# A two-layer diffusion transformer with product-key experts: weight splits taken from GpSimd, a norm's scales moved into the choice of experts, gathered rows written over more chunks, and a modulation read from PSUM by two engines

## The chip, the cores and the metric

The kernel runs on one core of one Trainium2 chip. The metric is device time in microseconds (us), the median over runs of the whole program. The core has five engines with queues of their own: TensorE (PE in the profile, PEld for its weight loads), VectorE (DVE), ScalarE (ACT), GpSimd (POOL) and SyncE (SP). Transfers between HBM and SBUF are issued on the queues of SP, POOL and ACT; one engine waits for another by semaphores.

## The reference, cut to what matters

Two streams of 256 tokens (the latents `x` and a context `ctx`) with 1024 features go through two layers. Layer 0's mixer is latent attention beside bidirectional retention, layer 1's is a gated delta rule. Each is followed by a layer of experts with product keys (`peer`), and both have a modulation ahead and a post-norm behind. Only the latents of layer 1 are returned.

```python
for l in range(2):
    mod = silu(c) @ ada_w[l] + ada_b[l]            # six vectors: shift, scale, gate, twice
    h = x * (1 + sc1) + sh1                        # modulate; the context with its own vectors
    y = attn_retention(h) if l == 0 else deltanet(h)
    x = layer_norm(ALPHA * x + g1 * y) * ln1_g[l] + ln1_b[l]
    f = peer(x * (1 + sc2) + sh2)
    x = layer_norm(ALPHA * x + g2 * f) * ln2_g[l] + ln2_b[l]

def peer(h):                                       # per block of 128 tokens, 8 heads
    q = (h @ w_q).reshape(128, 8, 2, 128)
    v1, i1 = top_k(q[:, :, 0] . k1, 16); v2, i2 = top_k(q[:, :, 1] . k2, 16)
    sc, j = top_k(v1[..., :, None] + v2[..., None, :], 16)   # over 16 x 16 sums
    e = i1[j] * 128 + i2[j]                        # one of 16384 experts
    return sum(softmax(sc) * gelu(u_tab[e] . h) * v_tab[e])
```

## The kernel before, in words

**Precision.** All large products are made in 32 bits from two halves: `split` (L262) writes a rounded high half with ScalarE (L268) and the remainder `x - hi` as low half with VectorE or, where a caller says so, GpSimd (L271); `mm3` (L256) makes three matmuls of the four halves. So each weight costs a load, one ScalarE pass and one VectorE or GpSimd pass.

**Order.** The program is written as Python generators that `weave` and `pipe` interleave; this is the order of the text. The framework beneath then orders the instructions of each engine with a planner of its own, which uses modelled durations and takes the order of the text as priority, and sets the semaphores. Each engine works through its own list in order.

**First mixer** (`mixer0`, L468). Sixteen column blocks of the input weights (128x1024 each) are loaded and split by `weights` (L494), whose low halves (`arwl`) are made by GpSimd; 24 matmuls of 512 columns use each. The value projection of the retention (`ret_v`, L606) loads four more weights (`rvw`) through the same helper. Woven beside the sixteen projections are 24 `ada_unit`s (L333) with two instructions each: products of VectorE over a 128x1024 tile (`adaj`, L341), which make the modulation vectors of layer 0. `ret_v` follows alone (L630). Later the eight weights of the output projection (`wout`, L780) are split, every third low half by GpSimd.

**Norm and modulation.** `norm` writes the normalized x without its scale and shift; `modulate` (L430) folds both into the modulation's own scale and shift. For each of eight feature blocks TensorE transposes x into PSUM, VectorE scales it into the tile `hf` (L445), ScalarE copies that into the high half (L446), and VectorE and GpSimd by turns make the low half (L447). So x itself still lacks its scale and shift, which the residual needs: `affine` (L424) applies them, as two passes of GpSimd over each 128x1024 block, with rows that `norm_rows` (L388) loads over POOL's queue.

**Choice of experts** (`route`, L813). For each of 16 half heads: a projection (weights `wq` split with GpSimd making `usl`), a product with the keys, then VectorE's top 16 of each block's scores; after each second one, four sums of candidates (`cand`, L883) and a top 16 over them. `choose` (L889) pairs the projections with the top 16s and steps the dense layer's early chunks between. Then the choice is decoded and spread into a dense table of weights W in HBM (`spread`), while the remaining early chunks run. The early chunks (36 of 128 in layer 0, 24 in layer 1) are the products of expert rows `u` with the tokens, which don't need W.

**Dense layer** (`Dense.run`, L1148). All 128 chunks of 128 experts are gone through: the product with `u` and gelu where it wasn't made early, gelu times w (a slice of W, L1172), the split of both and of `v`, and the product with `v` (tile `f`) accumulated in PSUM. In layer 0 it does three blocks of tokens. The fourth block has its 128 chosen rows per token gathered (`Rows.steps`, L1057): per step one indirect load of a row of `u` and one of `v` on POOL's queue, one product of VectorE with `u` (`rowu`, L1072) and one accumulation with `v` (`rowy`, L1082), with `v` eight steps behind; 136 steps in all.

**What fills the dense loop** (`build`, L1711 on). A dictionary `fill` says what is written ahead of which chunk. `at(share)` finds the chunk at a share of the cost, which counts 18 for an early chunk and 36 for another, over 122 chunks. The 136 steps lie between 0.9 times the early share and 1, the 48 `ada_unit`s of layer 1 between the early share and 0.97, the affine of layer 0's four blocks (`affine`, L1731, called through `fill` at 0.4) in the middle, and the preparation of the gates ahead of chunk 124. Layer 1's dense loop has its own `affine` for two blocks, ahead of chunk 2.

Of the kernel before, what the change touches and what calls it, by code (L numbers as in the profile page):

```python
# [10 lines left out]
F32 = mybir.dt.float32  # L11
# [231 lines left out]
class Model:  # L243
# [186 lines left out]
    def modulate(self, pool, ps, l, m, x, s, hs, i0, ln):  # L430
        nc = self.nc
        sl = slice(i0 * P, (i0 + 2) * P)
        g, b = (self.c["ln_c"][:, ln[0], ln[1] - 1, z, :] for z in range(2))
        sc = pool.tile([P, KD], F32, tag="msc", name=f"msc{l}{m}{s}", bufs=2)
        sh = pool.tile([P, KD], F32, tag="msh", name=f"msh{l}{m}{s}", bufs=2)
        nc.vector.tensor_mul(sc, self.mod[l, m + 1][:, :, s], g)
        nc.vector.tensor_mul(sh, self.mod[l, m + 1][:, :, s], b)
        nc.vector.tensor_add(sh, sh, self.mod[l, m][:, :, s])
        for k in range(KD):
            self.n += 1  # L440
            o = ps.tile([P, 512], F32, tag="ps", name=f"xt{self.n}")
            for i in range(2):
                nc.tensor.transpose(o[:, i * P:(i + 1) * P], x[2 * s + i][:, k * P:(k + 1) * P], self.c["ident"])
            t = pool.tile([P, T], F32, tag="hf", name=f"hf{self.n}", bufs=3)
            nc.vector.tensor_scalar(t, o[:, :T], sc[:, k:k + 1], sh[:, k:k + 1], ALU.mult, ALU.add)  # L445
            nc.scalar.copy(hs[0][:, k, sl], t)  # L446
            (nc.gpsimd if k % 2 else nc.vector).tensor_sub(hs[1][:, k, sl], t, hs[0][:, k, sl].bitcast(F32))  # L447

# [19 lines left out]
    def mixer0(self, open_x, open_h):  # L468
# [25 lines left out]
        def weights(src, shape, nm):  # L494
            w = pw.tile(shape, F32, tag="w", name=nm, bufs=2)
            nc.sync.dma_start(w, src)
            return self.split(pw, w, shape, "arw", eng=nc.gpsimd)

# [120 lines left out]
        with ExitStack() as e2:  # L619
            pa = self.pool(e2, "m0ada2", 1, side="right")  # L620
            self.silu_rows(pa)

            def units():
                for m in (2, 3, 4):
                    for k in range(KD):
                        self.ada_unit(pa, 0, m, k, (0, 1))
                        yield

            weave(low(), pipe([key()] + [ret_proj(j) for j in range(4, 16)], 2), units())
            weave(ret_v())  # L630
        ep.close()
# [142 lines left out]
        with ExitStack() as e2:  # L774
            p = self.pool(e2, "m0o", 1, side="right")
            w = []
            for k in range(KD):
                r = p.tile([P, D], F32, tag="woutr", name=f"woutr{k}", bufs=3)
                nc.sync.dma_start(r, a["ar_out"][:, k, :])
                w.append(self.split(p, r, [P, D], f"wout{k}", eng=nc.gpsimd if k % 3 == 2 else nc.vector))  # L780
                next(rest, None)
# [30 lines left out]

    def route(self, l, hs, parts, ps, first, dense, e2, rows=None):  # L813
        nc, a, c = self.nc, self.a, self.c
# [15 lines left out]
        kT = p.tile([P, 16, P], F32, tag="A", name=f"kT{l}")  # L830
        nc.sync.dma_start(kT, a["p_k"][l])

        def top16(pool, vals, v, i, n, nm):
# [55 lines left out]
        def choose(part):  # L889
# [6 lines left out]
            while True:  # L896
                ends = [next(g, pr) is pr for g in (pr, tp)]
                if all(ends):
                    return
                if ends[0]:  # L900
                    n += 1
                    step(1 + n % 2)
                yield

# [109 lines left out]
        for part in range(len(parts)):  # L1014
            weave(choose(part))
        eq_.close()
        dense.by = None
# [646 lines left out]
def build(nc, tc, a, out, dbg=None, upto="all"):  # L1664
    es = ExitStack()
    with es:
# [38 lines left out]
        dense = m.Dense(m, 0, h, 3, *pools0, EARLY[0])  # L1705
        wd = m.route(0, h, ((0, 1, 2, 3),), ps, first, dense, e2, rows)
        ep.close()
# [8 lines left out]
        fill = {}  # L1716
        cost = np.cumsum([18 if c < EARLY[0] else 36 for c in range(NE - 6)])

# [6 lines left out]
        for i, u in enumerate(units):  # L1725
            n = 3 * KD
            share = ahead_share * (0.1 + 0.9 * i / n) if i < n else ahead_share + (0.97 - ahead_share) * (i - n) / (len(units) - n)
            fill.setdefault(at(share), []).append(lambda u=u: m.ada_unit(pa, *u))
        kept = {}

        def affine():  # L1731
            rows = m.norm_rows(pa, 0, 1, "adat")
            for t in x[:4]:
                m.affine(nc.gpsimd, t, rows)

# [3 lines left out]

        fill.setdefault(at(0.4), []).append(affine)  # L1740
        fill[0] = [lambda: m.silu_rows(pa)]
        fill[124] = [prepare]
        for i in range(P + LAG):
# [21 lines left out]
        with ed:  # L1765
            ep, ps = phase("r1ps")
            dense = m.Dense(m, 1, h, 2, *pools1, EARLY[1])
            wd = m.route(1, h, ((0, 1),), ps, first, dense, e2)
            ep.close()
# [6 lines left out]

            def affine():
                rows = m.norm_rows(pn, 1, 1)
                for t in x[2:4]:
                    m.affine(nc.gpsimd, t, rows)  # L1780

            last = dense.run(wd, *pools, {2: [affine]})
            for tb in range(2):
# [20 lines left out]
```

## Time and profile before

The median of three runs is 3058.61 us (3046.81, 3058.61, 3059.09). The profiled execution took 3056.68 us, of which its span, from the first to the last instruction, is 3054.9.

| | of the span |
|---|---|
| profiled execution, its span | 3056.68 us, 3054.9 us |
| TensorE busy | 2773.7 us, 91%, 16867 matmuls |
| VectorE busy | 2249.5 us, 74% |
| ScalarE busy | 1291.4 us, 42% |
| GpSimd busy | 643.4 us, 21% |
| granted clock of TensorE, mean | 0.955 |
| moved by DMA | 643.85 MB, 211 GB/s |

The stages follow one another: the first mixer's start and projections until 190 us, attention and retention until 300, its output projection until 371 with norm and modulation, layer 0's choice until 502, its decoding and the early chunks until 722, layer 0's dense loop until 1700, norm and modulation until 1736, the delta rule until 2157, layer 1's choice from 2170 to 2240, its table until 2360, its dense loop until 3035, and the last norm. A share of the whole span is an average over stages of different limits, so each is read by itself. In the view by stretches the busy times stand in the order TensorE, its weight loads, VectorE, ScalarE, GpSimd, each with its instructions in brackets; a clock of 1.00 is TensorE's full clock. A busy time counts an instruction from start to end, waiting for a shared resource included: the same instruction can show different durations in different stages.

### The profile page before, as it was taken

What the parts mean: (1) busy time and instruction counts of PE and PEld (TensorE: products, weight loads), DVE (VectorE), ACT (ScalarE), POOL (GpSimd) and SP (SyncE); (2) the same over time, 40 slices, a digit from 0 to 9 for tenths busy, and PEclk for the clock granted to TensorE, in tenths of its full rate; (3) what the DMA queues carried; (4) which work ended last, traced back from release to release, by engine and by line L of the source; (5) the groups of instructions that cost most, each with busy time, mean ns of one, the idle gap of its engine ahead of it and who ended that gap; (6) DMA issues with size and microseconds to landing.
All of it is one profiled execution on the core that took longest, in us unless ns stands there. A gap on an engine that the chain in (4) does not pass through costs nothing.

```text
span 3054.9 us, 44722 instructions
## 1 busy us (share of the span) xinstructions
PE 2773.7 (91%) x16867; PEld 2412.5 (79%) x16867; DVE 2249.5 (74%) x4414; ACT 1291.4 (42%) x2176; POOL 643.4 (21%) x413
## 2 busy tenths in 40 slices
PE   7988898987999789999999899678878899999997
PEld 4766788986788688888899677667877689999996
DVE  2976599796999898999744578876898655555555
ACT  3335333674333233333333356333457454444443
POOL 2410134001036765666100000122400100000000
PEclk9999899998999999999999899788999999999999
DMA  6531223668999799999744123313348866666763
GB/s 231 186 121 45 95 89 109 232 236 318 325 360 390 284 400 374 394 397 395 250 153 135 57 73 94 91 56 119 117 152 296 262 221 207 215 213 207 214 206 110
DMA packets 272168, 643.85 MB, mean 211 GB/s; under 512 B 36464, under 2 KB 138992, under 8 KB 267472
## 3 DMA queue, kind: packets, MB, share of 16 engines
q1 hardware_dynamic: 225120, 487.50, 47.7%
q0 software_dynamic: 38768, 142.49, 12.0%
q10 hardware_dynamic: 8064, 11.01, 1.0%
q8 instruction: 132, 2.16, 0.3%
q14 instruction: 84, 0.69, 0.1%
HBM read 583.77 MB, written 57.15 MB: 210 GB/s over the span
## 4 chain that ended last, share of the span: by engine, by line
PE 35%; DVE 13%; issue 9%; DMA 8%; POOL 5%; ACT 3%; POOLq 0%; DVEq 0%; ACTq 0%; SPq 0%
PE f L254 14%; PE act L254 13%; DMA rowv<-p_v,rowe 3%; PE dz L254 3%; DMA vr<-p_v 2%; POOL rowv L1065 2%; POOL rowu L1065 2%; DMA ur<-p_u 1%; DVE usl L271 1%; DVE vsl L271 1%; DVE cv L1332 1%; DVE rowu L1072 1%; PE qb L254 1%; DVE adaj L341 1%; DVE rowy L1082 1%
## 5 line engine op out<-in xcount | busy, mean ns | idle before, releaser
L254 PE MATMUL f<-vsl,gsh 128*128 128x512 f32 x1260 | 498.2, 397 | 29.2 <-DVE vsl L271 29.1
L254 PE MATMUL f<-vsh,gsh 128*128 128x512 f32 x1260 | 488.8, 397 | 23.7 <-ACT vsh L268 11.9
L254 PE MATMUL f<-vsh,gsl 128*128 128x512 f32 x1260 | 494.2, 394 | 7.0 <-DVE gsl L271 7.0
L271 DVE TENSOR_TENSOR vsl<-vr,vsh 128x1024 fp32r<-128x1024 f32 x252 | 304.2, 1239 | 193.9 <-ACT vsh L268 193.4
L271 DVE TENSOR_TENSOR usl<-ur,ush 128x1024 fp32r<-128x1024 f32 x240 | 293.8, 1225 | 182.4 <-ACT ush L268 180.8
L268 ACT ACTIVATE ush<-ur 128x1024 fp32r<-128x1024 f32 x256 | 270.3, 1056 | 268.5 <-PE act L254 165.9
L254 PE MATMUL act<-hp0h,usl 128*128 128x384 f32 x1024 | 348.1, 340 | 19.2 <-DVE usl L271 12.4
L254 PE MATMUL act<-hp0h,ush 128*128 128x384 f32 x1024 | 349.1, 341 | 3.6 <-ACT ush L268 3.3
L254 PE MATMUL act<-hp0l,ush 128*128 128x384 f32 x1024 | 346.7, 339 | 0.0
L268 ACT ACTIVATE vsh<-vr 128x1024 fp32r<-128x1024 f32 x252 | 257.6, 1053 | 207.9 <-PE f L254 141.1
L268 ACT ACTIVATE gsh<-gelu 128x384 fp32r<-128x384 f32 (+1 forms) x256 | 120.4, 471 | 490.7 <-DVE gelu L1172 380.7
L254 PEld LDWEIGHTS f<-vsl,gsh 128*128 128x128 f32 x1260 | 240.1, 191 | 85.9 <-DVE vsl L271 39.5
L254 PEld LDWEIGHTS f<-vsh,gsh 128*128 128x128 f32 x1260 | 238.6, 191 | 81.7 <-ACT vsh L268 22.8
L254 PE MATMUL act<-hp1h,usl 128*128 128x256 f32 x1024 | 292.6, 286 | 8.3 <-DVE usl L271 8.3
L254 PE MATMUL act<-hp1h,ush 128*128 128x256 f32 x1024 | 293.2, 286 | 1.3 <-ACT ush L268 1.2
L254 PE MATMUL act<-hp1l,ush 128*128 128x256 f32 x1024 | 292.3, 285 | 0.0
L254 PEld LDWEIGHTS f<-vsh,gsl 128*128 128x128 f32 x1260 | 240.0, 190 | 58.1 <-DVE gsl L271 8.4
L1065 POOL DMA_INDIRECT rowu<-p_ur,rowe x128 | 173.9, 1358 | 272.6 <-DVE rowa L1072 180.1
L254 PEld LDWEIGHTS act<-hp0h,usl 128*128 128x128 f32 x1024 | 195.0, 190 | 21.5 <-DVE usl L271 13.7
L1065 POOL DMA_INDIRECT rowv<-p_v,rowe x128 | 190.8, 1490 | 100.0 <-DVE rowy L1082 77.3
L254 PEld LDWEIGHTS act<-hp1h,usl 128*128 128x128 f32 x1024 | 198.4, 194 | 9.4 <-DVE usl L271 9.2
L254 PEld LDWEIGHTS act<-hp1h,ush 128*128 128x128 f32 x1024 | 198.7, 194 | 3.8 <-ACT ush L268 1.7
(777 smaller groups left out, 5810.8 us busy)
## 6 DMA issues: line engine op xcount, KB each, us to landing
ur<-p_u SPq DMA_DIRECT2D x256, 512.0 KB
vr<-p_v SPq DMA_DIRECT2D x256, 512.0 KB
adat<-ada_t SPq DMA_DIRECT2D x80, 512.0 KB
W<-wst SPq DMA_DIRECT2D x20, 2048.0 KB
w<-W SPq DMA_DIRECT2D x32, 768.0 KB
wq<-p_wq SPq DMA_DIRECT2D x32, 512.0 KB
dw<-dn_in SPq DMA_DIRECT2D x32, 512.0 KB
w<-W SPq DMA_DIRECT2D x32, 512.0 KB
```

What stands on the lines that cost most here:

```text
L254: self.nc.tensor.matmul(out, l, r, start=start, stop=stop)
L268: nc.scalar.activation(hi, x, AF.Copy)
L271: (eng or nc.vector).tensor_sub(lo, x, hi.bitcast(F32))
L341: nc.vector.tensor_tensor_reduce(j, w, self.crow[:, s, :], op0=ALU.mult, op1=ALU.add, scale=1.0, scalar=self.c["ada_c"][:, l, m, k:k + 1], ...
L1065: nc.gpsimd.indirect_dma_start(t, None, tabs[z], bass.IndirectOffsetOnAxis(ap=self.e[:, s:s + 1], axis=0))
L1072: nc.vector.tensor_tensor_reduce(u, u, self.h, op0=ALU.mult, op1=ALU.add, scale=1.0, scalar=0.0, accum_out=self.act[:, s:s + 1])
L1082: nc.vector.scalar_tensor_tensor(self.y, rows.pop((1, v)), self.g[:, v:v + 1], self.y, ALU.mult, ALU.add)
L1332: (nc.gpsimd if CONV[j] == "p" else nc.vector).scalar_tensor_tensor(co, xp[:, :ns, q:q + T], cw[:, j, q:q + 1], co, ALU.mult, ALU.add)
```

## The change

In seven places:

1. `modulate`: ScalarE makes the high half from the transposed block in PSUM with scale and bias, instead of copying VectorE's result; VectorE makes all low halves.
2. `weights` in the first mixer: the low halves are made by VectorE (the default of `split`).
3. The `ada_unit`s of the first mixer: 16 of 24 are woven beside the projections, the rest three at a time beside `ret_v`.
4. The output weights: all low halves by VectorE.
5. `route` gets `x` and a generator `scaled`, which loads the scale and shift on POOL's queue and applies them to each block with GpSimd; `choose` takes one of its passes every fourth turn, and what is left is taken at the end. It runs in both layers.
6. The two `affine`s in `build` are gone.
7. The cost of `at` runs over 126 chunks instead of 122, the `ada_unit`s of layer 1 end at 0.87 instead of 0.97, and the entry at chunk 124 is added to what stands there.

```diff
@@ modulate
-            nc.scalar.copy(hs[0][:, k, sl], t)
-            (nc.gpsimd if k % 2 else nc.vector).tensor_sub(hs[1][:, k, sl], t, hs[0][:, k, sl].bitcast(F32))
+            nc.scalar.activation(hs[0][:, k, sl], o[:, :T], AF.Identity, bias=sh[:, k:k + 1], scale=sc[:, k:k + 1])
+            nc.vector.tensor_sub(hs[1][:, k, sl], t, hs[0][:, k, sl].bitcast(F32))
@@ mixer0
-            return self.split(pw, w, shape, "arw", eng=nc.gpsimd)
+            return self.split(pw, w, shape, "arw")
...
-            weave(low(), pipe([key()] + [ret_proj(j) for j in range(4, 16)], 2), units())
-            weave(ret_v())
+            sums = units()
+            weave(low(), pipe([key()] + [ret_proj(j) for j in range(4, 16)], 2), islice(sums, 2 * KD))
+            weave(ret_v(), until=sums, steps=3)
...
-                w.append(self.split(p, r, [P, D], f"wout{k}", eng=nc.gpsimd if k % 3 == 2 else nc.vector))
+                w.append(self.split(p, r, [P, D], f"wout{k}"))
@@ route
-    def route(self, l, hs, parts, ps, first, dense, e2, rows=None):
+    def route(self, l, hs, parts, ps, first, dense, e2, x, rows=None):
...
+        def scaled():
+            gb = p.tile([P, 2, D], F32, tag="A", name=f"lgb{l}")
+            for i, z in enumerate("gb"):
+                nc.gpsimd.dma_start(gb[:, i, :], a[f"ln1_{z}"][l])
+            for t in x:
+                nc.gpsimd.tensor_mul(t, t, gb[:, 0, :])
+                yield
+                nc.gpsimd.tensor_add(t, t, gb[:, 1, :])
+                yield
+
+        scale = scaled()
@@ choose
+                n += 1
                 if ends[0]:
-                    n += 1
                     step(1 + n % 2)
+                if n % 4 == 0:
+                    next(scale, None)
                 yield
...
             weave(choose(part))
+        weave(scale)
@@ build
-        wd = m.route(0, h, ((0, 1, 2, 3),), ps, first, dense, e2, rows)
+        wd = m.route(0, h, ((0, 1, 2, 3),), ps, first, dense, e2, x[:4], rows)
...
-        cost = np.cumsum([18 if c < EARLY[0] else 36 for c in range(NE - 6)])
+        cost = np.cumsum([18 if c < EARLY[0] else 36 for c in range(NE - 2)])
...
-            share = ahead_share * (0.1 + 0.9 * i / n) if i < n else ahead_share + (0.97 - ahead_share) * (i - n) / (len(units) - n)
+            share = ahead_share * (0.1 + 0.9 * i / n) if i < n else ahead_share + (0.87 - ahead_share) * (i - n) / (len(units) - n)
...
-        def affine():
-            rows = m.norm_rows(pa, 0, 1, "adat")
-            for t in x[:4]:
-                m.affine(nc.gpsimd, t, rows)
...
-        fill.setdefault(at(0.4), []).append(affine)
-        fill[124] = [prepare]
+        fill.setdefault(124, []).append(prepare)
...
-            wd = m.route(1, h, ((0, 1),), ps, first, dense, e2)
+            wd = m.route(1, h, ((0, 1),), ps, first, dense, e2, x[2:4])
...
-            def affine():
-                rows = m.norm_rows(pn, 1, 1)
-                for t in x[2:4]:
-                    m.affine(nc.gpsimd, t, rows)
-
-            last = dense.run(wd, *pools, {2: [affine]})
+            last = dense.run(wd, *pools, {})
```

## Rows read from the trace of the kernel before

**Rows 1.** Busy time by stretches: us, busy per engine (count), clock, DMA share, GB/s
```profile
70.00:180.00 110.00, 98.78 (x433) 80.37 (x432) 107.15 (x153) 32.14 (x44) 44.60 (x16) 0.95 0.53 179
384.00:502.00 118.00, 112.37 (x573) 97.91 (x571) 115.66 (x807) 37.62 (x55) 42.29 (x18) 0.99 0.26 86
1000.00:1070.00 70.00, 52.80 (x252) 46.75 (x250) 54.57 (x59) 15.94 (x23) 50.13 (x31) 0.91 0.75 272
1070.00:1480.00 410.00, 387.63 (x1906) 347.58 (x1907) 382.53 (x522) 138.01 (x207) 244.71 (x171) 0.97 1.02 387
1500.00:1690.00 190.00, 190.00 (x983) 173.83 (x982) 75.98 (x90) 70.44 (x97) 0.00 (x0) 1.00 0.46 143
```

**Rows 2.** Timeline of GpSimd, 1010 to 1070: start, us, line, instruction, [idle before, releaser]
```profile
1017.34 2.49 POOL L425 TENSOR_TENSOR x<-x,lg 128x1024 f32<-128x1024 f32 x1 [8.43 <-DMA lg<-ln_g]
...
1049.86 13.13 POOL L426 TENSOR_TENSOR x<-x,lb 128x1024 f32<-128x1024 f32 x4 [5.12 <-DMA lb<-ln_b]
```

**Rows 3.** Timeline of VectorE, 1046 to 1066
```profile
1050.69 6.74 DVE L271 TENSOR_TENSOR vsl<-vr,vsh 128x1024 fp32r<-128x1024 f32 x2
```

**Rows 4.** Groups by line of VectorE, 1070 to 1480: busy us, mean ns, idle before
```profile
L1082 DVE SCALAR_TENSOR_TENSOR rowy<-rowv,rowg,rowy 128x1024 f32<-128x1024 f32 x90 | 115.7, 1285 | 22.4 <-DMA rowv<-p_v,rowe 21.9 <-DVE rowg L1079 0.5
L1072 DVE CUSTOM_DVE_ANT_0 rowu<-rowu,rowh 128x1024 f32<-128x1024 f32 x85 | 103.8, 1221 | 0.0
...
L271 DVE TENSOR_TENSOR vsl<-vr,vsh 128x1024 fp32r<-128x1024 f32 x46 | 54.2, 1221 | 0.0
L341 DVE CUSTOM_DVE_ANT_0 adaj<-adat,c_row,small 128x1024 f16<-128x1024 f32 x21 | 26.9, 1279 | 0.0
L1172 DVE TENSOR_TENSOR gelu<-gelu,w 128x384 f32<-128x384 f32 x46 | 25.5, 554 | 7.0 <-ACT gelu L1137 7.0
```

**Rows 5.** Chain of waits, 2340 to 2400: start, us, what
```profile
2360.06 13.68 DMA w<-W
2373.76 5.41 DVE gelu L1172 x3
2379.17 2.49 DVE gsl L271
```

**Rows 6.** Timeline of GpSimd, 2350 to 2390
```profile
2371.55 4.85 POOL L425 TENSOR_TENSOR xl<-xl,lg 128x1024 f32<-128x1024 f32 x2 [8.81 <-DMA lg<-ln_g]
2376.36 5.01 POOL L426 TENSOR_TENSOR xl<-xl,lb 128x1024 f32<-128x1024 f32 x2
```

**Rows 7.** Timeline of VectorE, 2370 to 2390
```profile
2382.24 1.08 DVE L1172 TENSOR_TENSOR gelu<-gelu,w 128x256 f32<-128x256 f32 x3
```

**Rows 8.** Groups by line of GpSimd, 20 to 210
```profile
L271 POOL TENSOR_TENSOR arwl<-arw,arwh 128x1024 fp32r<-128x1024 f32 x16 | 43.2, 2699 | 92.9 <-ACT arwh L268 85.6 <-PE z L254 7.3
```

**Rows 9.** Groups by line of VectorE, 60 to 210
```profile
L341 DVE CUSTOM_DVE_ANT_0 adaj<-adat,c_row,small 128x1024 f16<-128x1024 f32 x48 | 79.1, 1648 | 13.5 <-ACT c_row L330 12.3 <-DMA adat<-ada_t 0.6
```

**Rows 10.** Instructions of L603: durations min/median/max in ns
```profile
L603 DVE TENSOR_TENSOR rq<-rq,rcos x4: 409/1340/2303, 105.1 to 128.7; 128x256 f32<-128x256 f32 x4
```

**Rows 11.** Who waited for tile arwl: us, times
```profile
  PE rvp L254: 3.2, 2
  PE z L254: 1.6, 1
```

**Rows 12.** Instructions of L883: durations min/median/max in ns
```profile
L883 DVE TENSOR_TENSOR cand<-V x64: 164/200/2419, 394.7 to 2234.3; 128x32 f32<-128x32 f32 x24, 128x64 f32<-128x64 f32 x16, 128x96 f32<-128x96 f32 x8, 128x48 f32<-128x48 f32 x8
```

**Rows 13.** Timeline of GpSimd, 2170 to 2185
```profile
2176.92 2.40 POOL L271 TENSOR_TENSOR usl<-wq,ush 128x1024 fp32r<-128x1024 f32 x1 [0.91 <-ACT ush L268]
```

**Rows 14.** Instructions of L447: durations min/median/max in ns
```profile
L447 DVE TENSOR_TENSOR hp0l<-hf,hp0h x16: 415/426/427, 349.7 to 1734.8; 128x256 fp32r<-128x256 f32 x16
L447 POOL TENSOR_TENSOR hp0l<-hf,hp0h x16: 715/732/1182, 350.2 to 1735.4; 128x256 fp32r<-128x256 f32 x16
```

**Rows 15.** Instructions of L513: durations min/median/max in ns
```profile
L513 ACT ACTIVATE h0h<-xT,mod,mod x16: 589/592/602, 45.9 to 53.3; 128x256 fp32r<-128x256 f32 x16
```

**Rows 16.** Busy time of tile rowy by stretch: DVE, POOL, clock, DMA share, GB/s
```profile
1500.00:1690.00 190.00, 0.00 (x0) 0.00 (x0) 1.00 0.46 143
```

## The prediction, made before the changed kernel was run

> **What bounds the kernel now.** I read the busy time by stretches first, then the groups by line inside each stretch, then the waits of one tile and the timeline where a group's mean hid a few long instructions. The profiled execution took 3056.68 us (its span is 3054.9), 1.9 us below the median of the runs, 3058.61; the sum is made against 3056.68.
>
> The stretches have different bounds [rows 1]. From 1500 to 1690, layer 0's dense loop without anything woven in, TensorE is busy 190.0 of 190 us at full clock: 983 matmuls, 5.17 per us. From 1070 to 1480, the same loop with the gathered rows, VectorE is busy 382.5 of 410 and TensorE makes 1906 matmuls, 4.65 per us: VectorE leads there. From 1000 to 1070 both fall: 252 matmuls, 3.60 per us, with the clock at 0.91. In layer 0's choice of experts (384 to 502) VectorE is busy 115.7 of 118. In the first mixer's projections (70 to 180) it is busy 107.2 of 110, TensorE 98.8.
>
> **Layer 0's scales leave the dense loop.** Eight GpSimd passes over a 128x1024 tile stand at 1017 to 1063: one alone 2.49 us (three more like it), the last four together 13.13 [rows 2], so 23 us. VectorE's instructions that run beside them are held: two vsl splits took 6.74 us [rows 3], where one takes 1.22 [rows 4]. From 1000 to 1070 TensorE made 73 matmuls fewer than at the rate of 1070 to 1480 (4.65 x 70 = 325 against 252), worth 73 / 4.65 = 15.8 us. So the gain lies between 15.8 (what TensorE shows inside the window) and 23 (all of GpSimd's passes, with the gathers queued behind them on POOL's queue). I take 20, past the middle, because the gathers delayed at 1063 cost a little behind the window too. The cover of this work is gone with it: what is late next is VectorE's own load, as in 1070 to 1480. **-20.**
>
> **Layer 1's scales leave its dense loop.** Here the passes sit on the chain of waits: w (the table of weights) lands at 2373.74 after 13.68 us, three gelu products take 5.41 us, one gsl 2.49, and GpSimd's four passes run from 2371.55 to 2381.4 [rows 5, 6]. Three such products without a neighbour take 1.08 us [rows 7], 0.36 each. So 5.41 - 1.08 = 4.3 and 2.49 - 0.36 = 2.1 go: 6.4. Two of the four 0.5 MB loads of scales issued beside w go as well, an estimate of 1.05 MB / 387 GB/s [rows 1] = 2.7 us. Between 6.4 and 9.1; below that if the next vr loads are late anyway. I take 8. **-8.**
>
> **The first mixer's splits.** Twenty weight splits of 128x1024 leave GpSimd (16 at a mean of 2.70 us [rows 8], and four more of the same shape) for VectorE, at 1.22 each as vsl [rows 4]: +24.4 us there. What VectorE gets back is its waiting beside GpSimd. Its 48 ada products have a mean of 1.648 us [rows 9] against 1.279 in the dense loop [rows 4]: 17.7 us; rotary products of 0.41 go up to 2.30 [rows 10]. So VectorE's sum changes by +6.7 or, with the rotary ones, by about nothing. TensorE's own waits for arwl are 3.2 and 1.6 us [rows 11] and go in part. Ends: +6.7 (VectorE's added time at the stage's end) and -11.2 (all of TensorE's idle time from 70 to 180 [rows 1]). I take the 4.8 less a little. Eight of the 24 ada units are written beside the v projection now; they are the filler of VectorE in either place. **-4.**
>
> **The choices get twelve passes.** Eight (layer 0) and four (layer 1), each some 2.4 us, and two 0.5 MB loads each on POOL's queue ahead of them. The first pass of x waited 8.43 us for its load [rows 2], and whatever stands behind it on POOL, the splits of wq that TensorE needs, waits too. VectorE's top-16 instructions read one tensor; those that read two can be held: a cand sum has a median of 0.20 us and a maximum of 2.42, a whole GpSimd pass [rows 12]. In layer 0 POOL is busy 42.3 of 118 us [rows 1] and 8 x 2.4 + 8.4 = 28 fit into the rest, with at most two cand sums held: 0 to +5. In layer 1 POOL has 0.91 us between splits [rows 13]: each pass pushes the next split by 2.4 - 0.9 = 1.5, four by 6, and the load's wait beyond one period of 3.3 adds 5: 0 to +11. VectorE sees it only when the scores come late, so I take a third of 16. **+5.**
>
> **Modulation.** Per stream of eight blocks, VectorE takes four more differences of 0.43 us, 1.7; GpSimd's, 0.73 each, leave [rows 14] the chain. ScalarE's instruction grows to that of 0.59 us with scale and bias [rows 15], and ScalarE has room (37.6 busy of 118 even beside it [rows 1]). Five streams: between +8.5 (all of VectorE's) and -6.0 (4 x 0.30 x 5). TensorE's k-by-k start hides most of either. **0.** The Trainium skill speaks against a gain here: "PSUM — Partial Sum Buffer", section "PSUM bank collisions raise a hardware error", says that two engines may not use one bank and quadrant at once, two reads included. By it ScalarE's read has to stand behind VectorE's of the same transposed block and the chain stays as long as it is; without it each stream would begin up to one scaling on VectorE earlier. No row shows two engines on one PSUM tile at a time.
>
> **Output weights.** Two of eight splits move (GpSimd to VectorE); that stretch waits for the loads. Between -1 and +2.4, taken as **0**.
>
> **Pacing.** The steps of the gathered rows were written at 136 over chunks 32 to 121, 1.5 per chunk. The trace has 90 rowy and 46 vsl in 410 us [rows 4]: 1.96 per chunk, and none after 1500 [rows 16], 19 chunks before the text's end. So the order on VectorE isn't that of the text: the framework's planner puts ready work that is written later into time that it counts as free. Four more chunks of text change nothing in that, nor does an ada share of 0.87 (21 units per 46 chunks in the trace, 18 as written). I take **0**; the other end is priced as the first rival, -41. A loss is bounded by the steps left over at the end, 2.6 us each.
>
> **Sum.** -20 - 8 - 4 + 5 + 0 + 0 + 0 = -27: 3056.7 - 27 = 3029.7, **3030 us**. With each term at its nearer end, 3015 to 3043.
>
> **Rivals.**
> *The pacing holds.* If the steps stay where they are written, two chunks of VectorE cost 2 x (1.22 + 1.22 + 0.55 + 0.55) = 7.1, 2.9 steps x (1.285 + 1.221 + 0.08) = 7.5, 0.84 ada x 1.36 = 1.1 [rows 4]: 15.7 us, under TensorE's 2 x 42 matmuls / 5.17 = 16.2. Then 1070 to 1480 runs at TensorE's rate: 410 - 1906 / 5.17 = 41.3 go [rows 1]. Time: 2988. Against it: the rate of 1.96, the same before and after the pause at 1000. 12%.
> *The choices eat it.* The twelve passes land on VectorE's chain at their full 16 us, and layer 1's gain shrinks to 4 because its loop is then fed late: 3030 + 11 + 4 = 3045. For: POOL's 0.91 us in layer 1, and the wait of 8.43 for a load that the planner had not foreseen. Against: in layer 0 VectorE consumes slower (118 / 16 = 7.4 us per head half) than POOL's queue supplies (42.3 / 16 = 2.6 now, 4.4 with the passes and the load's wait). 22%.
> *VectorE becomes the bound of the first mixer.* It is busy 107.2 of 110 us already. If each projection's low half is ready only after one ada product and its own split, 1.28 + 1.22 = 2.5 us past TensorE's need, 20 x 2.5 = 50 us are lost instead of 4 gained: 3030 + 54 = 3084, slower than before. It decides as soon as the split starts later than the third matmul of its projection; today's two splits of lead (24 matmuls each, 24 x 98.78 / 433 = 5.5 us [rows 1]) speak against it, VectorE's in-order queue for it. 9%.
> The forecast itself has 57%.
>
> **How the numbers follow.** About 0.5%, 15 us, is what can be told from no change here: faster is below 3043, slower above 3074. The forecast's 57% and the paced rival's 12% lie below, less some 3% of the forecast's upper tail, plus 2% of the second rival: 68% faster. The second rival's rest and that tail: 22% the same (1% to the rival's other side). The third rival and mishaps: 10% slower. The range takes in the paced rival and the second one, 2986 to 3054, and leaves out the third and the tails; the forecast's own range is 3015 to 3043.
>
> **What would show it.** Right: no POOL pass inside the two dense loops; 1000 to 1070 at 4.6 matmuls per us; gelu products of 0.36 us at the start of layer 1's loop; ada products at 1.28 in the first mixer; some 4 rowy per two chunks still, ending about 19 chunks before the loop does. Wrong: rowy present up to the last chunks (first rival); idle VectorE in the choices ended by ScalarE's S (second); TensorE's idle time in 70 to 180 ended by VectorE's arwl (third). The prediction as a whole is wrong if the loop of 1070 to 1480 changes its rate, since every other term is small beside that.

## The result

The changed kernel takes 3023.64 us (median of 4 runs, 3018.56 to 3027.8) against 3058.85 before: a ratio of 0.9891 with a 95% interval of 0.9866 to 0.9915. Predicted were 3030, in a range of 2986 to 3054, and faster with 68%. The profiled execution took 3025.72 us with a span of 3024.0, 30.9 below the span of before.

To see where they went, the traces are cut at the same instructions of TensorE. The table is worked out from the start times of its first or last matmul into the tile named in brackets (`rvp` belongs to the value projection, `q` to the attention, `xt` to the transposes of the modulation, `pq` to the choice of experts, `f` to the dense layer, `dz` and `yo` to the delta rule). The column of before has the length of each stage in us; every other entry is the length of that stage less its length before, so that a row with the same number in several kernels is one effect. The kernels E1 to E12 are the experiments below.

| stage, from its first to the next one's first matmul | before | after | E1 | E2 | E3 | E4 | E5 | E6 | E7 | E12 |
|---|---|---|---|---|---|---|---|---|---|---|
| start and 16 projections (to `rvp`) | 157.9 | -4.7 | +0.5 | -4.4 | -0.8 | +1.5 | -3.8 | -5.4 | -5.3 | -4.0 |
| value projection (to `q`) | 30.4 | -7.3 | +0.4 | -7.3 | 0 | -0.1 | -7.3 | -7.3 | -7.3 | -7.3 |
| attention, output projection (to `xt`) | 159.7 | +2.0 | -0.3 | +1.3 | 0 | +2.7 | +3.2 | +3.1 | +0.9 | +1.4 |
| norm, modulation of layer 0 (to `pq`) | 20.4 | +6.7 | 0 | 0 | +1.4 | 0 | 0 | 0 | +1.5 | +6.4 |
| choice, table (to `f`) | 359.0 | -1.3 | +3.9 | -4.9 | -3.8 | -5.3 | -5.5 | +5.4 | -0.2 | -4.3 |
| dense loop of layer 0 (to `dz`) | 1009.0 | -18.8 | -18.3 | +5.1 | +4.0 | +2.2 | +5.1 | -20.4 | -10.6 | -60.4 |
| delta rule (to the last `yo`) | 412.7 | +2.4 | +1.4 | +1.8 | +3.8 | +0.6 | +2.5 | +1.9 | -0.5 | +0.9 |
| norm, choice, table of layer 1 (to `f`) | 225.7 | -1.7 | +0.3 | -1.0 | -2.1 | +0.3 | +5.5 | +1.2 | -6.8 | -2.1 |
| dense loop of layer 1 (last `f`) | 662.4 | -7.8 | -4.0 | -1.7 | -1.3 | +0.7 | -0.9 | -7.1 | -6.5 | -7.3 |
| rest | 17.9 | -0.4 | -0.4 | -0.2 | -0.2 | -0.2 | -0.2 | -0.4 | -0.2 | -0.4 |

E8, E9, E10 and E11, which the table leaves out, have +76.1, +54.9, +55.5 and +73.6 in the dense loop of layer 0.

How far one execution can be trusted is read from the columns whose edit lies elsewhere. E2 to E5 all have 4 to 6 us less between `pq` and `f` and 2 to 5 more in the loop behind: the border between these two stages lay late in the one execution of before, and their sum, 1368.0, moves by no more than 3.1 in them. The rows of layer 1 vary by up to 5.5, and the attention by 2.7 in E4, whose edit lies behind it.

Now the views of the kernel after. The busy time by stretches, where the fourth to last column is GpSimd (with instructions), then clock, DMA share and GB/s, answers to [rows 1]:

```profile
996.00:1066.00 70.00, 67.02 (x336) 59.81 (x335) 66.67 (x90) 25.04 (x38) 41.24 (x31) 1.00 1.04 398
1066.00:1476.00 410.00, 388.02 (x1918) 346.48 (x1918) 375.99 (x509) 138.04 (x206) 226.10 (x164) 0.99 1.00 376
1476.00:1666.00 190.00, 190.00 (x984) 173.81 (x983) 75.85 (x90) 70.40 (x97) 0.00 (x0) 1.00 0.45 143
```

In the 70 us that answer to 1000 to 1070 TensorE makes 336 matmuls, 4.80 per us instead of 3.60, at a clock of 1.00 instead of 0.91: GpSimd's passes are gone from there. The next 410 us are as they were, 1918 matmuls against 1906. The tile `rowy` is as empty at the loop's end as in [rows 16]:

```profile
1476.00:1666.00 190.00, 0.00 (x0) 0.00 (x0) 1.00 0.45 143
```

In layer 1 the first gelu products take 0.36 us each, where three took 5.41 [rows 5]; VectorE's timeline:

```profile
2351.02 1.09 DVE L1189 TENSOR_TENSOR gelu<-gelu,w 128x256 f32<-128x256 f32 x3
```

The passes went further forward than the text has them. The timelines of GpSimd and of VectorE at layer 0's second modulation, in columns as in [rows 2]:

```profile
356.29 4.83 POOL L840 TENSOR_TENSOR x<-x,lgb 128x1024 f32<-128x1024 f32 x2 [3.26 <-ACT x L421]
361.08 5.02 POOL L842 TENSOR_TENSOR x<-x,lgb 128x1024 f32<-128x1024 f32 x2
366.06 5.08 POOL L840 TENSOR_TENSOR x<-x,lgb 128x1024 f32<-128x1024 f32 x2
375.36 2.40 POOL L271 TENSOR_TENSOR usl<-wq,ush 128x1024 fp32r<-128x1024 f32 x1 [4.22 <-ACT ush L268]
```

```profile
356.07 1.45 DVE L445 TENSOR_SCALAR hf<-xt,msc,msh 128x256 f32<-128x256 f32 x3 [1.84 <-PE xt L443]
357.43 6.45 DVE L447 TENSOR_TENSOR hp0l<-hf,hp0h 128x256 fp32r<-128x256 f32 x3
363.80 1.44 DVE L445 TENSOR_SCALAR hf<-xt,msc,msh 128x256 f32<-128x256 f32 x3
365.16 6.26 DVE L447 TENSOR_TENSOR hp0l<-hf,hp0h 128x256 fp32r<-128x256 f32 x3
```

The text puts the first pass into the choice, which starts at 365.0; GpSimd made it at 356.3, as soon as x was normalized. Three differences of VectorE take 6.45 us beside them, 2.15 each, against 0.43 [rows 14], and TensorE's first projection waits 7.5 us. The Trainium skill ("SBUF — State Buffer", section "Summary: rules for kernel authors") says that of a VectorE instruction with two inputs in SBUF and a GpSimd one that reads SBUF the later waits until the other is done; these durations agree, each about one GpSimd pass of 2.4 us.

### The profile page after: what moved, and what is told of

Read it like the earlier page. It is cut to its first block, busy times and chain, and to the rows that moved or that the text cites. A ratio compares the mean times of both kernels' runs of the same rounds, so it can differ in the third digit from the quotient of the medians.

```text
span 3024.0 us, 44724 instructions
## 1 busy us (share of the span) xinstructions
PE 2772.1 (92%) x16867; PEld 2411.1 (80%) x16867; DVE 2242.3 (74%) x4456; ACT 1293.5 (43%) x2176; POOL 552.2 (18%) x371
## 4 chain that ended last, share of the span: by engine, by line
PE 38%; DVE 13%; DMA 11%; issue 8%; ACT 4%; POOL 3%; POOLq 0%; SPq 0%; ACTq 0%; DVEq 0%
PE f L254 15%; PE act L254 14%; DMA rowv<-p_v,rowe 3%; DMA ur<-p_u 3%; PE dz L254 3%; DMA vr<-p_v 3%; POOL rowv L1082 1%; POOL rowu L1082 1%; DVE vsl L271 1%; DVE usl L271 1%; DVE rowu L1089 1%; DVE rowy L1099 1%; DMA w<-W 1%; DVE cv L1349 1%; PE wp L254 1%
## 5 line engine op out<-in xcount | busy, mean ns | idle before, releaser
L254 PEld LDWEIGHTS act<-hp1l,ush 128*128 128x128 f32 x1024 | 199.1, 194 | 2.8 <-issue 0.6
```

What stands on the lines that cost most here:

```text
L254: self.nc.tensor.matmul(out, l, r, start=start, stop=stop)
```

## The experiments

All times are medians, and the ratios are to the kernel before on the same chip. They are named E1 to E12 in the order of their labels.

**E1, the scales alone.**

```diff
-        fill.setdefault(at(0.4), []).append(affine)
...
-            last = dense.run(wd, *pools, {2: [affine]})
+            last = dense.run(wd, *pools, {})
...
+                if n % 4 == 0:
+                    next(scale, None)
```

> Of the change only the move of the scales from the two dense loops into the two choices, everything else as before. Theory (read from the two traces): the passes run earlier than the text has them, beside the second modulation of layer 0, and hold VectorE's low halves there: the time from the first transposed block to the first projection of the choice grows by 7 us (it grew from 20.4 to 27.2 with the whole change), layer 0's dense loop loses 19 to 20, layer 1's choice grows by 2 to 5, layer 1's dense loop loses 11; in all -20 from 3058 = 3038. Rival: those 7 us come from the modulation's own edit; then that stretch stays at 20.4 here and the whole is -27 = 3031.

3038.05 us, ratio 0.9924 (0.9902 to 0.9946). The total is what the theory said, 3038, but its terms are not. The stretch to `pq` stays at 20.4, which was the rival's sign, so the 7 us there need a second edit; and layer 1 has -4.0 in its loop and +0.3 in its choice, where -11 and +2 to +5 were expected. Here the passes run at 378.9 and later, in the choice, and TensorE pays there. The timeline of GpSimd, then TensorE's waits (us, times, longest):

```profile
378.90 4.75 POOL L839 TENSOR_TENSOR x<-x,lgb 128x1024 f32<-128x1024 f32 x2 [5.16 <-DMA lgb<-ln_g]
383.61 4.66 POOL L841 TENSOR_TENSOR x<-x,lgb 128x1024 f32<-128x1024 f32 x2
388.22 2.34 POOL L839 TENSOR_TENSOR x<-x,lgb 128x1024 f32<-128x1024 f32 x1
390.51 2.34 POOL L271 TENSOR_TENSOR usl<-wq,ush 128x1024 fp32r<-128x1024 f32 x1
```

```profile
PE pq L254 <- POOL usl L271: 9.0, 2, 8.8
```

The split `usl` at 390.51 stands behind five passes on GpSimd's queue, and the projection that needs it waits 8.8 us. The eight passes cost about as much as in the changed kernel (+3.9 in the choice, against +6.7 - 1.3 = 5.4 for both stages there); only the victim is another.

**E2, the first mixer alone** (its splits and the order of the units).

```diff
-            return self.split(pw, w, shape, "arw", eng=nc.gpsimd)
+            return self.split(pw, w, shape, "arw")
...
-            weave(low(), pipe([key()] + [ret_proj(j) for j in range(4, 16)], 2), units())
-            weave(ret_v())
+            sums = units()
+            weave(low(), pipe([key()] + [ret_proj(j) for j in range(4, 16)], 2), islice(sums, 2 * KD))
+            weave(ret_v(), until=sums, steps=3)
```

> Of the change only the first mixer: its twenty weight splits by VectorE and the order of the 24 units. Theory: the gain of 12 us up to the last matmul of the value projection (10 up to the output projection) belongs to this part alone, 4.7 of it ahead of the value projection; the rest of the program keeps its length: 3058 - 10 = 3048. Rival from the prediction (VectorE becomes the bound): the projections end later, above 3060.

3046.28 us, ratio 0.9956 (0.9942 to 0.9969). The theory holds: 11.7 us less up to `q`, and the rival that VectorE becomes the bound is out.

**E5, the splits without the order of the units.**

```diff
-            return self.split(pw, w, shape, "arw", eng=nc.gpsimd)
+            return self.split(pw, w, shape, "arw")
```

> Of the change only the twenty splits of the first mixer by VectorE; the 24 units all stay beside the projections. With splits and units together the last matmul of the value projection came 11.8 us earlier, 4.4 of it ahead of that projection and 7.4 in it. Theory: the 7.4 come from the splits (TensorE waited there for GpSimd's arwl), so here too the value projection takes 21.5 instead of 28.9 us, and the whole is 3061 - 10 = 3051. Rival: the order of the units makes them; then the projections end later here with 24 units in them, and at least 5 of the 11.8 us are gone: 3056 or more.

3051.73 us, ratio 0.9962 (0.9938 to 0.9986). Its first two stages, -3.8 and -7.3, are within 0.6 of those of E2 (-4.4 and -7.3): the splits make the gain. The 0.6 is less than what the first row moves by in E3 and E4, whose edits lie elsewhere (-0.8 and +1.5), so a gain by the order of the units isn't shown.

**E3, the modulation alone.**

```diff
-            nc.scalar.copy(hs[0][:, k, sl], t)
-            (nc.gpsimd if k % 2 else nc.vector).tensor_sub(hs[1][:, k, sl], t, hs[0][:, k, sl].bitcast(F32))
+            nc.scalar.activation(hs[0][:, k, sl], o[:, :T], AF.Identity, bias=sh[:, k:k + 1], scale=sc[:, k:k + 1])
+            nc.vector.tensor_sub(hs[1][:, k, sl], t, hs[0][:, k, sl].bitcast(F32))
```

> Of the change only the modulation: ScalarE makes the high half from PSUM, VectorE all low halves. Theory: 0 within 1 us in each of the three places (first transposed block to first projection stays 20.4 +- 1 in layer 0), the whole 3058 +- 5; ScalarE's instruction on a block begins only when VectorE's on the same block has ended. Rival: this edit is what took 7 us ahead of layer 0's choice: that stretch is 27 here and the whole 3065.

3063.49 us, ratio 1.0011 (0.9993 to 1.0029): no difference. The stretch is 1.4 longer, not 7 (and 1.5 longer in E7, which has this edit and no passes there). ScalarE's group in it (mean ns, idle time, releaser):

```profile
L446 ACT ACTIVATE hp0h<-xt,msh,msc 128x256 fp32r<-128x256 f32 x16 | 7.9, 560 | 12.0 <-DVE hf L445 12.0
```

All of the 12.0 us that ScalarE waited ahead of these sixteen instructions ended with VectorE's `hf`. It reads PSUM and no longer reads `hf`, and still it starts behind VectorE's read of the same block; before, when it did read `hf`, it waited 11.1 us for it. The wait is one for a semaphore, so the run shows that the program orders the two reads, and not what the chip would do without that order. This order agrees with the rule that the prediction cites from the Trainium skill ("PSUM — Partial Sum Buffer", section "PSUM bank collisions raise a hardware error").

**E6, everything but the modulation.**

```diff
+            nc.scalar.copy(hs[0][:, k, sl], t)
+            (nc.gpsimd if k % 2 else nc.vector).tensor_sub(hs[1][:, k, sl], t, hs[0][:, k, sl].bitcast(F32))
```

> The changed kernel with the modulation of before. Theory: it is the two edits together that put GpSimd's passes into the second modulation, since GpSimd has no low half of its own left to wait for; with its low halves back, the stretch from the first transposed block to the first projection is 20.4 us again (27.2 in the changed kernel) and the passes run in the choice, where they cost as much: the whole within 4 us of the changed kernel, 3020 to 3028. Rival: the 7 us are gained for good: 3016.

3026.92 us, ratio 0.9882 (0.9846 to 0.9917). The theory holds: with low halves of its own in GpSimd's queue the stretch is back at 20.4, and the choice and table take 5.4 more instead of 1.3 less: TensorE's longest wait there, 9.2 us, is again for a split `usl` of GpSimd.

**E4, the pacing alone.**

```diff
-        cost = np.cumsum([18 if c < EARLY[0] else 36 for c in range(NE - 6)])
+        cost = np.cumsum([18 if c < EARLY[0] else 36 for c in range(NE - 2)])
...
-            share = ... + (0.97 - ahead_share) * ...
+            share = ... + (0.87 - ahead_share) * ...
```

> Of the change only the chunks ahead of which the gathered rows and the units of layer 1 are written. Theory (the planner decides, not the text): the last rowy stays at chunk 101 +- 1, 1070 to 1480 keeps 4.65 to 4.70 matmuls per us, the whole 3058 +- 5. Rival (the pacing holds): rowy up to chunk 125, 5.1 matmuls per us, 3017.

3060.06 us, ratio 0.9994 (0.9977 to 1.0011). The last `rowy` stands at chunk 101, as before and after, and 1070 to 1480 has 1890 matmuls, 4.61 per us, against 4.65 before. The edit does nothing that can be told. The ratios of E1 to E4 multiply to 0.9885, and the whole change has 0.9891: within their intervals the parts add up, although two of them, the scales and the modulation, pay their price in another place when they are together. The edit of the output weights was not run by itself.

**E7, the passes put late into both dense loops**, on the changed kernel.

```diff
+                nc.vector.tensor_scalar_mul(t[:, :4], dense.g[max(dense.g)][:, :4], 0.0)
+                nc.sync.dma_start(t, a[f"ln1_{z}"][0])
...
+        fill.setdefault(105, []).append(affine)
...
+            last = dense.run(wd, *pools, {40: [affine]})
```

> The changed kernel with the passes taken out of the choices and put where TensorE leads and VectorE has room: behind the last gathered row in layer 0 (from chunk 105), and at chunk 40 in layer 1, their loads held until that chunk's gelu by a small write of VectorE into the same tile. Theory: the choices and the stretch ahead of layer 0's lose 8 to 10 us in layer 0 and 2 to 5 in layer 1, the dense loops lose nothing: 3024 - 11 = 3013. Rival: GpSimd holds VectorE there too and TensorE runs dry, 12 passes of 2.4 us: 3024 - 11 + 29 = 3042.

3021.22 us, ratio 0.9885 (0.9832 to 0.9937): not to be told from the changed kernel. The stretch and the choice get cheaper by 4.1 (+1.5 and -0.2 for +6.7 and -1.3), the loop of layer 0 gains 8.2 less. The timeline of GpSimd shows the passes at 1493 to 1515, and TensorE's waits from 1500 to 1560 what they cost:

```profile
1492.78 5.76 POOL L425 TENSOR_TENSOR x<-x,lglate 128x1024 f32<-128x1024 f32 x2 [40.41 <-DMA lglate<-ln_g]
...
1510.52 4.74 POOL L426 TENSOR_TENSOR x<-x,lblate 128x1024 f32<-128x1024 f32 x2
```

```profile
PE act L254 <- DVE usl L271: 2.3, 1, 2.3
PE f L254 <- DVE vsl L271: 0.4, 1, 0.4
```

That is 2.7 us; another 3.0 were lost at 832, in a wait for ScalarE's `vsh`, of which the changed kernel has 1.5 there, and the rest is within what single executions differ by. So the passes cost some us wherever VectorE has two-input work, and this version is not shown to be better than the changed kernel.

**E8, rows that can't come early**, on the changed kernel: the index of each four rows is copied with a term that needs the gelu of the chunk.

```diff
+                    c = max(dense.g)
+                    nc.vector.scalar_tensor_tensor(t, dense.g[c][:, :4], 0.0, self.f[:, 4 * q:4 * q + 4], ALU.mult, ALU.add)
```

> The changed kernel with gathered rows that really follow the text: the index of each four rows is copied by VectorE from a table with a factor that needs the gelu of the chunk ahead of which the step stands, so the gather can't be issued earlier. Theory (VectorE's crowding by rows that come early is what slows chunks 36 to 101): rowy then ends at chunk 117, VectorE takes 15.7 us per two chunks against TensorE's 16.5, and the loop of layer 0 gains 25 to 41 us: 2983 to 2999. Rival: the DMA share of 1.02 or the waits between gather and product set the rate and not VectorE's order; then the loop is as long as before or longer: 3024 or more.

3113.6 us, ratio 1.0163 (1.0124 to 1.0203). **E9** makes the index two groups ahead; **E10** is E9 with the rows written up to 0.92 of the cost and the passes late, as in E7 (from chunk 118 in layer 0):

```diff
+                if s % 4 == 0 and s + RING[0] + 4 * 2 < P:
+                    index(s + RING[0] + 4 * 2)
```

> As e8_paced, but the index of each four rows is made two groups (eight steps) ahead of where it is used, so that a gather is held back to the text and still has its row there before VectorE's product comes. e8 lost 90 us because VectorE stood in order in front of rows that had just been asked for (75 of 400 us of idle time ended by a transfer of rowu). Theory (VectorE's crowding is what slows chunks 36 to 101 in the changed kernel): that idle time goes, rowy ends at chunk 111, the loop gains 15 to 41 us against the changed kernel: 2983 to 3009. Rival (the rows' rate is bound by transfers and their waits, and early rows are what keeps the loop fed): 3024 or more.

> e9 with the rows written up to 0.92 of the cost and the scales' passes behind them, as in e7 (from chunk 118 in layer 0, 40 in layer 1). Theory: 3 to 5 us under e9, as e7 under the changed kernel. Rival: the last rows and the passes meet at the end of layer 0's loop and the norm behind it waits: 5 us above e9.

E9 3090.76 us, ratio 1.0099 (1.0071 to 1.0127); E10 3100.68, 1.0125 (1.0105 to 1.0145): the late passes give nothing there either. All three were expected to gain, E8 and E9 against the changed kernel and E10 against E9, and none did. VectorE's waits from 1100 to 1500, E8 first, then E9:

```profile
DVE rowu L1101 <- DMA rowu<-p_ur,rowx: 75.4, 35, 5.8
DVE rowy L1111 <- DMA rowv<-p_v,rowe: 19.6, 13, 2.0
```

```profile
DVE rowu L1103 <- DMA rowu<-p_ur,rowx: 69.4, 35, 5.6
DVE rowy L1113 <- DMA rowv<-p_v,rowe: 20.1, 12, 3.1
```

In the changed kernel no `rowu` waits in that time. VectorE, in order, now stands in front of rows on their way, 69 us even with the lead, while the DMA share falls from 0.96 to 0.84 and 0.86. That the indices, made in fours, let the gathers go out in bunches fits the 35 waits, but no run tests it. So these three tell that this way of pacing loses more than it can gain; whether rows spread over all chunks without bunching would gain stays open.

**E11 and E12, which resource holds chunks 36 to 101.** Both are the changed kernel with a part of the fourth block's work left out. In E11 VectorE's two instructions of a row work on 512 of 1024 columns, and the rows are fetched whole. In E12 half of each row is fetched, and VectorE's two instructions read that half twice.

```diff
-nc.vector.tensor_tensor_reduce(u, u, self.h, ...
+nc.vector.tensor_tensor_reduce(u[:, :512], u[:, :512], self.h[:, :512], ...
...
-nc.vector.scalar_tensor_tensor(self.y, rows.pop((1, v)), ...
+nc.vector.scalar_tensor_tensor(self.y[:, :512], rows.pop((1, v))[:, :512], ...
```

> The changed kernel with both instructions of a gathered row on 512 of its 1024 columns (the other half of the fourth block's sums is left out); the rows are fetched whole. VectorE has 1.2 us less per step, the transfers are the same; the planner then ends the rows at chunk 83 instead of 101. Theory of the prediction (VectorE's load is what holds chunks 36 to 101): layer 0's dense loop gains 25 to 41 us, whole 2983 to 2999. Rival (transfers hold it, the DMA share is 1.02 there): the rows come denser and the loop gains less than 10 us, 3014 or more.

```diff
-            tabs = m.a["p_ur"], m.a["p_v"][0].rearrange("n p d -> (n p) d")
+            tabs = m.a["p_ur"].rearrange("n (h d) -> (n h) d", h=2), m.a["p_v"][0].rearrange("n p (h d) -> (n p h) d", h=2)
...
-nc.gpsimd.indirect_dma_start(t, None, ...
+nc.gpsimd.indirect_dma_start(t[:, :512], None, ...
```

> The changed kernel with gathers of 512 instead of 1024 columns (half of each row is left out and the other half read twice), VectorE's instructions as long as before and in the same order, rows up to chunk 101. Transfers fall by some 1 MB per step to 0.5. Theory of the prediction (VectorE): the loop's length stays within 8 us, 3016 to 3028. Rival (transfers): chunks 36 to 101 go to TensorE's rate of 5.1 matmuls per us, 25 to 41 us less, 2983 to 2999.

E11 takes 3118.44 us, ratio 1.019 (1.0157 to 1.0223), E12 2980.73, 0.9731 (0.97 to 0.9762). Less work for VectorE makes the loop slower, less to transfer makes it faster by the whole excess. The busy time by stretches of the kernel after, E11 and E12:

```profile
1000.00:1450.00 450.00, 426.28 (x2108) 380.39 (x2107) 418.95 (x573) 153.81 (x229) 261.52 (x189) 0.99 1.02 386
```

```profile
1000.00:1400.00 400.00, 337.54 (x1539) 296.73 (x1539) 275.11 (x503) 111.53 (x173) 217.99 (x186) 0.91 1.01 385
```

```profile
1000.00:1420.00 420.00, 419.98 (x2132) 383.03 (x2131) 412.66 (x562) 151.68 (x223) 267.20 (x185) 1.00 0.85 291
```

In the changed kernel the DMA share is 1.02 at 386 GB/s. In E12 it is 0.85 at 291 GB/s, VectorE is as busy as in the changed kernel (412.7 of 420, its instructions on a row still 1.22 and 1.28 us long, the last row still at chunk 101), and TensorE is never idle: 5.08 matmuls per us instead of 4.68. In E11 the planner, which sees a shorter VectorE, ends the rows at chunk 83; the share stays at 1.01 while VectorE is busy for 275.1 of 400 only, and waits for rows in flight (E11's waits of VectorE in the same 400 us):

```profile
DVE rowy L1099 <- DMA rowv<-p_v,rowe: 51.9, 41, 3.5
DVE rowu L1089 <- DMA rowu<-p_ur,rowe: 33.6, 31, 2.0
```

So transfers hold this stretch, and VectorE's high share is beside the point. Whether it is their bytes or their packets isn't told apart: in E12 the gathers' queue moves 75.4 MB in 22384 packets instead of 142.5 in 38768.

The bound by transfers also gives the size of E11's loss. An estimate from these rows: behind the last row a chunk takes TensorE 8.1 us (42 matmuls, at 983 in 190 us) and brings 8.1 us x 143 GB/s = 1.16 MB, which is 3.0 us at 385 GB/s. When the rows end 18 chunks earlier, 18 chunks that cost 3.0 us each beside the rows cost 8.1 each behind them: 18 x 5.1 = 92 us. The loop is 92.4 us longer than in the changed kernel (+73.6 against -18.8).

## Why the prediction was right, and where not

The outcome lies 6.4 us from the forecast, and the change measures -30.9 by the spans where -27 was predicted. The stages say which terms carried it. (The forecast's own range, 3015 to 3043, can't be worked back from the terms: the ends that they give add up to 3006 on one side and 3068 on the other.)

**Layer 0's scales, -20: right.** The loop lost 18.8 (E1 18.3, E6 20.4), between the two bounds. Against E2 to E5, whose loop is 2 to 5 longer than before's, it is 21 to 24, about the upper bound of 23: all of GpSimd's passes. What the border between the two stages adds here it takes from the choice, below. From 1000 to 1075 TensorE waited 9.3 us for two `vsl` and 11.1 for a `usl` of VectorE before; from 996 to 1066 after it waited 3.0.

**Layer 1's scales, -8: right.** -7.8 in the loop, by the step named: the products at its start are at 0.36 us, and TensorE's waits there fall from 8.3 us to 0.7. E1's loop has only 4.0, although its waits at the start are as short (0.5); the rest of that difference stays open.

**The first mixer, -4: the direction right, the term mis-sized.** 12.0 us went up to `q`. The attention behind is 2.0 longer, but it is 2.7 longer in E4 too, so no loss is shown there. The measured -12.0 lies at the prediction's lower end of -11.2, all of TensorE's idle time there, for two reasons. First, the step took only the waits that [rows 11] ascribe to `arwl`, 4.8. TensorE's waits before and after:

```profile
PE cqb L254 <- ACT gcols L362: 6.1, 1, 6.1
PE rvp L254 <- POOL arwl L271: 3.2, 2, 2.0
PE rvp L254 <- ACT arwh L268: 1.6, 1, 1.6
PE z L254 <- POOL arwl L271: 1.6, 1, 1.6
```

```profile
PE cqb L254 <- ACT gcols L362: 2.2, 1, 2.2
PE z L254 <- DVE arwl L271: 0.4, 1, 0.4
```

The largest, 6.1 us in front of `cqb`, is put down to ScalarE, but falls to 2.2 when GpSimd stops, in E5 too. ScalarE's input comes from VectorE, in order behind an `adaj` that took 3.29 us instead of 1.28 beside a split of GpSimd (79.04, 2.37 us long):

```profile
79.20 3.29 DVE L341 CUSTOM_DVE_ANT_0 adaj<-adat,c_row,small 128x1024 f16<-128x1024 f32 x1
```

That is 2.0 of the 3.9 us by which the wait falls; the rest isn't traced. Second, the value projection's own matmuls ran at a clock of 0.94, with means of 410 to 416 ns; without the waits it is 1.00 and 389. One of its three groups before and after:

```profile
L254 PE MATMUL rvp<-arwl,h0h 128*128 128x512 f32 x32 | 13.3, 416 | 3.2 <-POOL arwl L271 3.2
L254 PE MATMUL rvp<-arwl,h0h 128*128 128x512 f32 x32 | 12.4, 389 | 0.0
```

So of the 7.3 us gained in this projection 4.8 are waits and about 2.4 the clock (its three groups took 39.6 us and take 37.2). VectorE's 48 `adaj` are now at 1.279 us, as the prediction had it from [rows 4, 9]:

```profile
L341 DVE CUSTOM_DVE_ANT_0 adaj<-adat,c_row,small 128x1024 f16<-128x1024 f32 x48 | 61.4, 1279 | 6.1 <-ACT c_row L330 3.5 <-DMA adat<-ada_t 2.3
```

**The choices, +5: near in sum by luck, wrong in place.** The table's entries add up to 3.7: 6.7 - 1.3 = 5.4 in layer 0 and -1.7 in layer 1. But layer 0 paid 5.4 only against before; against E2 to E5, whose choice is 4 to 6 shorter than before's, it paid 9 to 11. What doesn't hang on that border is the sum of layer 0's three stages, 6.7 - 1.3 - 18.8 = -13.4 (E1 -14.4, E6 -15.0), where -20 and 0 to +5 were predicted. In layer 1 nothing stands out (-1.7, E1 +0.3, E6 +1.2, in a row that moves by 5.5). The step bounded layer 0 by 5 from the room in GpSimd's queue within the choice. What decided was where the planner puts a pass: into the modulation ahead, when GpSimd has nothing else there, or in front of a split. The prediction used the planner's freedom for the rows and forgot it here. Its second rival, the full 16 in the choices, did not come.

**Modulation, output weights, pacing, 0 each: right** (E3 and E4; for the output weights no difference is seen between `q` and `xt` with their edit, +3.1 in E6, and without it, +3.2 in E5).

**The bound of the loop: wrong, without effect on the sum.** "VectorE leads there" failed: E12 shows transfers. The share of 1.02 stood in the row that was quoted for VectorE [rows 1], and [rows 4] has 21.9 us of waiting for `rowv`. The first rival, pacing that holds, priced the loop without the excess at -41; E12's is 41.6 below the changed kernel's, so its price was right, and its reason, VectorE's share, was not. The runs that did pace the rows, E8 to E10, lost.

## What to carry to other kernels

An engine's share near 1 does not name the bound when a second resource is at 1 too: halve each by itself, and see which one moves the time. Work that is ready early, on an engine that has room, is put where the planner likes; its price is then paid where its neighbours are, so price it at every place that it can reach. And a wait put down to one engine can be another's: follow what released it one step further.

## What had not been expected of the hardware

Where GpSimd's passes made TensorE wait, its granted clock was lower as well: 0.94 in the value projection and 0.91 at 1000 to 1070 before, 1.00 in both after. The value projection before had the lower of the clock's two levels, 1.2 of 2.4 GHz, from 169.3 to 172.7, behind a wait of 2.0 us. So there the waits came dearer than their length. And fewer columns per row made the program slower (E11): the rows' same bytes, at the same 385 GB/s, were through after fewer chunks, and more chunks were left to run behind them.
